# K transposed before its split, softmax reciprocals through DRAM, and gate work moved beside another product, in a two-layer encoder kernel

## The chip, the cores and the metric

The kernel runs on one core of a Trainium2 chip, as one program. The metric is the device time of one execution in microseconds (us). Times of before are the median of three runs; the profile is of one further execution of the same program.

## The reference, cut to what matters

Two layers of an encoder are applied to 1024 prompt tokens and 256 sample tokens (model width 1024, head width 64, all float32). In every layer a normalised, modulated input goes through head groups, an output projection, and a squared-ReLU MLP of width 4096.

```python
def gqa_full(q, k, v):
    ...
    def block(qblk):
        s = jnp.einsum('bqhgd,bkhd->bhgqk', qblk, k,
                       preferred_element_type=jnp.float32) * (Dh ** -0.5)
        p = jax.nn.softmax(s, axis=-1)
        return jnp.einsum('bhgqk,bkhd->bqhgd', p, vf)
```

Layer 0 has dilated-window attention (heads A) and grouped-query attention (heads B); both end as exp(scores) times V, divided by a row sum. Layer 1 has a bidirectional mLSTM (heads C) and a gated MLP over 128-token chunks (heads D): per token an input gate and a forget gate (running sums and maxima over the sequence), an output gate `sigmoid(o)` on the normalised mLSTM output, and `gelu(u) * mixed(v)` in D.

## The kernel before, in words

All 1280 tokens lie in NT = 10 tiles of P = 128 tokens. PE products of float32 data are made of three passes over a high and a low half (`split`, L91: ACT rounds to the high half, DVE subtracts to get the low one; names end in h and l): high by high, low by high, high by low. Weights come in raw through SP's DMA queue and are split the same way, on DVE or, where a caller asks, on POOL (`w_piece`, L269). The program is laid out by a scheduler from the order in which the code issues work; `after(...)` (L82) keeps what is issued within it behind named instructions, on all engines. Each engine then runs its own list in order.

The stages, with their place in the span: `start` (norms, layer-0 projections, and the K of heads B), `attention0` (366 to 806 us), `mix_out(0)` (output projection), `mlp_up(0)`, `mlp_down(0)` (to about 1757), `proj1` (layer-1 projections, 1757 to 2115), `mlstm` (to 2251), `mix_out(1)` (to about 2400), `mlp_up(1)` and `mlp_down(1)`.

**K.** For each tile `k_split` (L334) lays K out twice side by side on POOL, its high half first and then, by a subtraction, its low half. `k_trans` (L341) transposes both halves of both heads (four transposes by the identity, `M<-ident,kd`) and copies the high ones out on ACT (L349, `KH`), the low ones on DVE (L350, `KL`). That is 10 tiles in `start` and 40 in `attention0`.

**Attention items.** There are 80 items, one for each token tile and pair of query heads: 40 of heads B, then four units of 10 of heads A; the last two tiles of every ten are the short sample ones. For an item, `scores` (L566) makes scores and their exponentials with row sums, `trans` (L608) transposes the exponentials (L615, `T<-ident,pe`) and takes the reciprocals of the two sums (L623, `rc`), and `pv` (L627) multiplies by V into the PSUM tile `O`, of which there is one; DVE multiplies by the reciprocals (L648, `ot`) and a DMA stores the result (L650, `oT`). The three steps of an item are issued one item apart. The reciprocals stand one to a token, on partitions, and are needed along a row: POOL copies them out to 128 columns (L625, `rb`), PE transposes (L638), ACT copies to `rs` (L640). `mix_out(0)` loads the stored rows as its operand (L823).

**mlp_up.** Four pairs of weight groups q. Pairs 2 and 3 use a seven-product scheme; `up(P, w, x)` (L858) makes one product, 12 matmuls of 512 columns (4 blocks by three passes). S1 to S4 are sums of weights which DVE makes and splits (`w_sums` L980, `prepare` L999), and T1 to T4 are sums of the input.

**proj1.** `chunks` (L287) walks through specs in order: v (256 columns), og (output gates, 512 columns, L307), vg (gate inputs and D's values, 544 columns, L314), u (512 columns, L359), each over 10 tiles, 24 matmuls of 512 columns to a tile for og and u. In `vg`'s wake stand the mixing of D (L1335, transposes of `scr`) and the gates of C (`gates` L1426): a long chain on DVE of adds, scans (L1473 to L1497), exponentials on ACT and small products on PE (L1535, `tr<-R,selp`, decays). It is a generator of which `u` takes three steps per tile.

**mlstm and mix_out(1).** `w_out` (L713) is a generator of weight pieces for the next output projection; `weights(t)` (L1698) takes one at t = 0, 2, 4 and 6, and POOL makes their low halves. In `mix_out(1)`, `split(t)` (L748) splits the projection's operand (`hTh`, `hTl`), squares and sums the mLSTM output, and multiplies with the gates; at t = 0 the first half of the product and then the four weight pieces that are left are issued.

Of the kernel before, what the change touches and what calls it, by code (L numbers as in the profile page):

```python
# [9 lines left out]
F32 = mybir.dt.float32  # L10
# [39 lines left out]
class Trunk:  # L50
# [283 lines left out]
    def k_split(self, kd, k):  # L334

        src = k.rearrange("p (h d) -> p h d", d=HD).unsqueeze(2).to_broadcast([P, 2, 2, HD])
        self.nc.gpsimd.tensor_copy(kd[:, :, 0].bitcast(F32R), src)
        self.nc.gpsimd.tensor_sub(kd[:, :, 1], src, kd[:, :, 0])
        return kd

    def k_trans(self, kd, ps, K, t):  # L341

        nc = self.nc
        ps = ps.rearrange("p (b n) -> p b n", n=P)
        for h in range(2):
            for i in range(2):
                nc.tensor.transpose(ps[:, 2 * i + h], kd[:, h, i].rearrange("p a d -> p (a d)"), self.ident)
        sl = slice(t * P, (t + 1) * P)
        nc.scalar.activation(K[0][:, :, sl], ps[:, 0:2], AF.Copy, scale=-0.125)  # L349
        nc.vector.tensor_scalar(K[1][:, :, sl], ps[:, 2:4], -0.125, None, op0=OP.mult)  # L350
# [4 lines left out]
    def start(self):  # L355
# [4 lines left out]
        with ExitStack() as s:  # L360
# [95 lines left out]
            def kvb(t, z):  # L456
                z = z[0]
                r = norm(z[:, :P], 2)
                a = self.rope(z[:, :P], tabs["cosBk"], tabs["sinBk"], 2, 16, t)
                scaled(a, r, 2)  # L460
                kds[t] = self.k_split(t2p.tile([P, 2, 2, 2, HD], F32, name="kd", bufs=3), a[:, :P])
                for u in ([t - 2] if t > 1 else []) + ([t - 1, t] if t == NT - 1 else []):
                    self.k_trans(kds[u], self.ps("tr"), self.KB, u)
                v = self.t2()
                nc.scalar.activation(v[:, :P], z[:, P:2 * P], AF.Copy)
                nc.sync.dma_start(self.zd["vb"][:, t], v[:, :P])
# [31 lines left out]
    def attention0(self):  # L498
        nc, I, tc = self.nc, self.I, self.tc
        self.oT = [self.dram.tile([P, KB, P], F32, name=f"oT{t}") for t in range(NT)]  # L500
        with ExitStack() as s:
# [22 lines left out]
            def k_unit(u):  # L524
# [9 lines left out]
                def step(t, kt):  # L534
                    self.k_trans(self.k_split(ap.tile([P, 2, 2, 2, HD], F32, name="kd"), kt), self.ps("M"), K, t)
                    if t in (3, 7):
                        h = t // 4
                        off = 96 * (1 - h)
                        for X in K:
                            b = X.rearrange("p h (b n) -> p h b n", n=P)  # L540
                            for i in range(2):
                                nc.gpsimd.tensor_copy(b[:, i, NT + h].rearrange("p (c n) -> p c n", n=32),
                                                      self.f(b[:, i, 4 * h:4 * h + 4, off:off + 32]))
# [64 lines left out]
            def trans(it, h):  # L608
# [11 lines left out]
                if h == 1:  # L620
                    rc = ap.tile([P, 2], F32, name="rc", bufs=4)
                    for i in range(2):
                        nc.vector.reciprocal(rc[:, i:i + 1], it["sum", i])  # L623
                    rb = it["rb"] = ap.tile([P, 2, HD], F32, name="rb2", bufs=2)
                    nc.gpsimd.tensor_copy(rb, rc.unsqueeze(2).to_broadcast([P, 2, HD]))  # L625

            def pv(it):  # L627
# [9 lines left out]
                r = self.ps("M")  # L637
                nc.tensor.transpose(r[:, :P], it["rb"].rearrange("p h d -> p (h d)"), self.ident)  # L638
                rs = ap.tile([P, P], F32, name="rs", bufs=2)
                nc.scalar.activation(rs, r[:, :P], AF.Copy)  # L640
# [7 lines left out]
                nc.vector.tensor_mul(ot, o[:, :P], rs)  # L648
# [5 lines left out]
            for i, it in enumerate(items):  # L654
                it["last"] = i >= len(items) - 2
# [79 lines left out]
    def mix_out(self, l):  # L735
        nc = self.nc
        with ExitStack() as s:
# [10 lines left out]
            def split(t):  # L748
# [5 lines left out]
                else:  # L754
# [3 lines left out]
                    nc.scalar.activation(sq.rearrange("p (b n) -> p b n", b=4), o, AF.Square)  # L758
# [4 lines left out]
                    v = self.rawp.tile([P, 1088], F32, name="raw", bufs=4)[:, :512].rearrange("p (b n) -> p b n", b=4)  # L763
                    nc.vector.tensor_mul(v.rearrange("p b (h d) -> p b h d", d=HD), ov,
                                         r.rearrange("p (b h) -> p b h", h=2).unsqueeze(3).to_broadcast([P, 4, 2, HD]))
                    nc.vector.tensor_mul(v, v, g)
                    st["v", t] = v
                if t == 0:
                    if l == 1:
                        mm(0, range(4))  # L770
                    for _ in self.w_out:
                        pass
# [102 lines left out]
    def mlp_up(self, l):  # L875
# [6 lines left out]
        with ExitStack() as s:  # L882
# [161 lines left out]
            for q in range(2, self.N_PAIRS):  # L1044
# [37 lines left out]
                P5 = self.ps("u")  # L1082
# [6 lines left out]
                P3 = self.ps("u")  # L1089
                self.up(P3, w("S4"), mov["B22"])  # L1090
                nc.vector.tensor_add(C12, C12, P3)
# [182 lines left out]
    def proj1(self, keep):  # L1274
# [5 lines left out]
        with ExitStack() as s:  # L1280
# [26 lines left out]
            def og(t, z):  # L1307

                o = t2()
                nc.scalar.activation(o, z[0], AF.Sigmoid)  # L1310
                nc.gpsimd.tensor_mul(o, o, mh)
                nc.sync.dma_start(self.ogd[t * P:(t + 1) * P], o)

# [45 lines left out]
            def u(t, z):  # L1359
# [4 lines left out]
                if t == 0:  # L1364
                    late.pop("mix")()
                else:
                    u_trans(t - 1)
                for _ in range(3):
                    next(gen["g"], None)

            def u_trans(t):
                x = late.pop(("u", t))
                ps = self.ps("tr").rearrange("p (b n) -> p b n", n=P)
                for b in range(4):
# [6 lines left out]
            specs = [(w[:, 1280:1536], 256, None, v), (w[:, 1536:2048], 512, None, og),  # L1381
                     (I["w_vg"], 544, None, vg), (w[:, 2080:2592], 512, load_mix, u)]
# [3 lines left out]
            for _ in gen["g"]:  # L1386
                pass
# [164 lines left out]
    def mlstm(self):  # L1552
# [3 lines left out]
        with ExitStack() as s:  # L1556
# [141 lines left out]
            def weights(t):  # L1698
                if t % 2 == 0 and t < 8:
# [156 lines left out]
```

## Time and profile before

| | us |
|---|---|
| median of 3 runs | 3194.86 |
| lowest and highest run | 3188.7, 3201.8 |
| profiled execution, its own time | 3196.31 |
| its span, first to last instruction | 3194.5 |

| engine | busy us | share | instructions |
|---|---|---|---|
| PE | 3111.5 | 97% | 18045 |
| DVE | 1880.6 | 59% | 3339 |
| ACT | 1429.1 | 45% | 2905 |
| POOL | 784.7 | 25% | 828 |

The first two engines' shares are of the whole span. Time in a view is counted from the span's start. In a row of a timeline, the bracket at the end gives the time for which the engine was idle before, and the instruction that ended the wait. The granted TensorE clock (PEclk) is given as a share of the full 2.4 GHz; 0.50 is 1.2 GHz. Its mean over the span is 0.988.

### The profile page before, as it was taken

How to read it: one execution, taken by the hardware profiler on the slowest of the kernel's cores; microseconds unless marked ns; L12 is line 12 of the kernel's file. 1: busy time of each engine (PE TensorE's matmuls, PEld its weight loads, DVE VectorE, ACT ScalarE, POOL GpSimd, SP SyncE). 2: the span in 40 equal slices, each digit the busy share in tenths (PEclk: the TensorE clock that was granted, in tenths of full speed). 3: DMA queues.
4: the chain of work that ended last, by engine and by line, in shares of the span. 5: the costliest groups of instructions: out<-in, count | busy, mean ns of one | idle time of the engine just before them, and what ended most of it. 6: DMA issues, size and time to landing. Idle time of an engine off the chain costs nothing. (4 is left out here: it accounts for less than half of the span.)

```text
span 3194.5 us, 49043 instructions
## 1 busy us (share of the span) xinstructions
PE 3111.5 (97%) x18045; PEld 2582.4 (81%) x18045; DVE 1880.6 (59%) x3339; ACT 1429.1 (45%) x2905; POOL 784.7 (25%) x828
## 2 busy tenths in 40 slices
PE   7999999999999999999999999999899999999998
PEld 4777788888777888888888896889777888888887
DVE  4632266667668767644488135137678767654556
ACT  3411366677444444443366235125454444443344
POOL 2421122353005455400000221202014455500000
PEclk8999999999999999999999999999899999999999
DMA  8536622121634666765567313212643666675567
GB/s 271 170 131 213 198 75 80 47 70 48 208 99 159 218 216 224 249 211 172 177 212 235 111 54 102 63 39 67 182 164 122 215 223 223 228 243 172 177 217 230
DMA packets 312789, 520.42 MB, mean 163 GB/s; under 512 B 43093, under 2 KB 172293, under 8 KB 312421
## 3 DMA queue, kind: packets, MB, share of 16 engines
q1 hardware_dynamic: 312405, 516.89, 49.8%
q8 instruction: 142, 2.33, 0.3%
q14 instruction: 98, 0.80, 0.1%
q0 software_dynamic: 144, 0.39, 0.0%
HBM read 359.71 MB, written 157.48 MB: 162 GB/s over the span
## 5 line engine op out<-in xcount | busy, mean ns | idle before, releaser
L1133 PE MATMUL d<-w1l,sh 128*128 128x512 f32 x1120 | 436.4, 390 | 1.0 <-DVE w1l L94 1.0
L1134 PE MATMUL d<-w1h,sl 128*128 128x512 f32 x1120 | 436.0, 389 | 0.0
L1132 PE MATMUL d<-w1h,sh 128*128 128x512 f32 x1120 | 435.4, 389 | 0.0
L94 DVE TENSOR_TENSOR w1l<-raw,w1h 128x512 fp32r<-128x512 f32 x444 | 363.2, 827 | 119.4 <-ACT w1h L93 116.6
L864 PE MATMUL u<-hTh,w1l 128*128 128x512 f32 (+1 forms) x1056 | 359.2, 340 | 8.5 <-DVE w1l L94 8.5
L94 DVE TENSOR_TENSOR sl<-sraw,sh 128x640 fp32r<-128x640 f32 (+2 forms) x240 | 192.2, 802 | 296.2 <-ACT sh L93 295.9
L864 PE MATMUL u<-hTh,w1h 128*128 128x512 f32 (+1 forms) x1056 | 359.5, 340 | 3.3 <-ACT H L1018 1.7
L864 PE MATMUL u<-hTl,w1h 128*128 128x512 f32 (+1 forms) x1056 | 359.3, 340 | 0.1
L93 ACT ACTIVATE w1h<-raw 128x512 fp32r<-128x512 f32 x444 | 274.6, 622 | 140.3 <-PE u L864 102.7
L93 ACT ACTIVATE sh<-sraw 128x640 fp32r<-128x640 f32 (+2 forms) x240 | 168.6, 704 | 373.4 <-PE d L1133 348.6
L283 PE MATMUL z<-wh,hTh 128*128 128x512 f32 (+2 forms) x800 | 277.4, 364 | 2.1 <-ACT wh L93 1.0
L283 PE MATMUL z<-wl,hTh 128*128 128x512 f32 (+2 forms) x800 | 271.3, 356 | 1.1 <-DVE wl L94 0.5
L285 PE MATMUL z<-wh,hTl 128*128 128x512 f32 (+2 forms) x800 | 270.7, 355 | 1.6 <-DVE hTl L165 1.6
L1133 PEld LDWEIGHTS d<-w1l,sh 128*128 128x128 f32 x1120 | 210.2, 188 | 45.6 <-DVE w1l L94 1.8
L1132 PEld LDWEIGHTS d<-w1h,sh 128*128 128x128 f32 x1120 | 210.3, 188 | 43.5
L1134 PEld LDWEIGHTS d<-w1h,sl 128*128 128x128 f32 x1120 | 210.3, 188 | 43.2
L864 PEld LDWEIGHTS u<-hTh,w1l 128*128 128x128 f32 x1056 | 201.6, 191 | 32.0 <-DVE w1l L94 10.2
L864 PEld LDWEIGHTS u<-hTh,w1h 128*128 128x128 f32 x1056 | 201.8, 191 | 27.0 <-ACT w1h L93 2.1
L864 PEld LDWEIGHTS u<-hTl,w1h 128*128 128x128 f32 x1056 | 201.7, 191 | 22.6 <-DVE hTl L165 1.1
L94 POOL TENSOR_TENSOR wl<-raw,wh 128x1024 fp32r<-128x1024 f32 (+1 forms) x22 | 51.4, 2343 | 526.1 <-ACT wh L93 505.6
L940 POOL TENSOR_TENSOR raw<-raw 128x512 f32<-128x512 f32 x32 | 43.6, 1363 | 543.6 <-DMA raw<-in_w_ff 446.6
L283 PEld LDWEIGHTS z<-wh,hTh 128*128 128x128 f32 x800 | 146.3, 190 | 36.8 <-issue 9.1
(377 smaller groups left out, 6563.6 us busy)
## 6 DMA issues: line engine op xcount, KB each, us to landing
raw<-in_w_ff SPq DMA_DIRECT2D x128, 512.0 KB, 4.1
sraw<-hd SPq DMA_DIRECT2D x192, 320.0 KB, 3.1
wada<-in_w_ada SPq DMA_DIRECT2D x44, 1024.0 KB, 5.4
hd<-H SPq DMA_DIRECT2D x64, 640.0 KB, 4.5
wd<-raw SPq DMA_DIRECT2D x64, 512.0 KB, 3.0
raw<-in_w_ff SPq DMA_DIRECT2D x128, 256.0 KB, 3.8
raw<-wd SPq DMA_DIRECT2D x128, 256.0 KB, 3.2
hd<-part SPq DMA_DIRECT2D x96, 320.0 KB, 3.2
```

Source lines behind the costliest of these rows:

```text
L93: self.nc.scalar.activation(hi, src, AF.Copy)
L94: (eng or self.nc.vector).tensor_sub(lo, src, self.f(hi))
L283: nc.tensor.matmul(o, hi[:, k, sl], w[k][i][:, c], start=first and i == 0, stop=False)
L285: nc.tensor.matmul(o, lo[:, k, sl], w[k][0][:, c], start=False, stop=last)
L864: self.nc.tensor.matmul(o, a[:, k], b, start=(start and k == 0 and i == 0), stop=(stop and k == 3 and i == 2))
L940: v.tensor_sub(B11, B12, B11)
L1132: nc.tensor.matmul(ps, o[0][:, sl], w[0], start=first, stop=False)
L1133: nc.tensor.matmul(ps, o[0][:, sl], w[1], start=False, stop=False)
L1134: nc.tensor.matmul(ps, o[1][:, sl], w[0], start=False, stop=last)
```

## The change

K is laid out twice unsplit, transposed with two transposes, and split behind them: KH is copied out as before, KL is the scaled PSUM less KH. The reciprocals are written to DRAM by a DMA and come back by two broadcast reads as a row for each head. `v` of `mix_out(1)` has other buffers, and the weight pieces left at t = 0 are held behind t = 0's Square and gating product. In `mlp_up`'s pair 2 the product S1 by T1 stands behind S4 by B22. The output gates become 1 / (1 + exp(-o)) by ACT, DVE and DVE. `vg` stands before `og`, the mixing and the gates' steps go beside `og`, and what is left of the gates is issued at `u`'s first tile. The weight pieces in `mlstm` are taken at t = 0, 1, 2 and 3.

```diff
@@ -333,7 +333,5 @@
 
-    def k_split(self, kd, k):
+    def k_twice(self, kd, k):
 
-        src = k.rearrange("p (h d) -> p h d", d=HD).unsqueeze(2).to_broadcast([P, 2, 2, HD])
-        self.nc.gpsimd.tensor_copy(kd[:, :, 0].bitcast(F32R), src)
-        self.nc.gpsimd.tensor_sub(kd[:, :, 1], src, kd[:, :, 0])
+        self.nc.gpsimd.tensor_copy(kd, k.rearrange("p (h d) -> p h d", d=HD).unsqueeze(2).to_broadcast([P, 2, 2, HD]))
         return kd
@@ -343,9 +341,8 @@
         nc = self.nc
-        ps = ps.rearrange("p (b n) -> p b n", n=P)
+        ps = ps[:, :2 * P].rearrange("p (b n) -> p b n", n=P)
         for h in range(2):
-            for i in range(2):
-                nc.tensor.transpose(ps[:, 2 * i + h], kd[:, h, i].rearrange("p a d -> p (a d)"), self.ident)
+            nc.tensor.transpose(ps[:, h], kd[:, h].rearrange("p a d -> p (a d)"), self.ident)
         sl = slice(t * P, (t + 1) * P)
-        nc.scalar.activation(K[0][:, :, sl], ps[:, 0:2], AF.Copy, scale=-0.125)
-        nc.vector.tensor_scalar(K[1][:, :, sl], ps[:, 2:4], -0.125, None, op0=OP.mult)
+        nc.scalar.activation(K[0][:, :, sl], ps, AF.Copy, scale=-0.125)
+        nc.vector.scalar_tensor_tensor(K[1][:, :, sl], ps, -0.125, self.f(K[0][:, :, sl]), op0=OP.mult, op1=OP.subtract)
 
@@ -460,3 +457,3 @@
                 scaled(a, r, 2)
-                kds[t] = self.k_split(t2p.tile([P, 2, 2, 2, HD], F32, name="kd", bufs=3), a[:, :P])
+                kds[t] = self.k_twice(t2p.tile([P, 2, 2, HD], F32, name="kd", bufs=3), a[:, :P])
                 for u in ([t - 2] if t > 1 else []) + ([t - 1, t] if t == NT - 1 else []):
@@ -534,3 +531,3 @@
                 def step(t, kt):
-                    self.k_trans(self.k_split(ap.tile([P, 2, 2, 2, HD], F32, name="kd"), kt), self.ps("M"), K, t)
+                    self.k_trans(self.k_twice(ap.tile([P, 2, 2, HD], F32, name="kd"), kt), self.ps("M"), K, t)
                     if t in (3, 7):
@@ -623,4 +620,8 @@
                         nc.vector.reciprocal(rc[:, i:i + 1], it["sum", i])
-                    rb = it["rb"] = ap.tile([P, 2, HD], F32, name="rb2", bufs=2)
-                    nc.gpsimd.tensor_copy(rb, rc.unsqueeze(2).to_broadcast([P, 2, HD]))
+
+                    d = self.dram.tile([2, P], F32, name=f"rc{it['i'] % 4}")
+                    nc.sync.dma_start(d.rearrange("h p -> p h"), rc)
+                    rs = it["rs"] = ap.tile([P, P], F32, name="rs", bufs=3)
+                    for h in range(2):
+                        nc.sync.dma_start(rs[h * HD:(h + 1) * HD], d[h:h + 1].to_broadcast([HD, P]))
 
@@ -636,6 +637,2 @@
                     vb = [4 * hq + c for c in range(4)] + [4 * (1 - hq) + cq, NT + 1 - hq]
-                r = self.ps("M")
-                nc.tensor.transpose(r[:, :P], it["rb"].rearrange("p h d -> p (h d)"), self.ident)
-                rs = ap.tile([P, P], F32, name="rs", bufs=2)
-                nc.scalar.activation(rs, r[:, :P], AF.Copy)
                 o = self.ps("O")
@@ -647,3 +644,3 @@
                 ot = kp.tile([P, P], F32, name="ot", bufs=2)
-                nc.vector.tensor_mul(ot, o[:, :P], rs)
+                nc.vector.tensor_mul(ot, o[:, :P], it["rs"])
                 q = nc.gpsimd if it["last"] else nc.sync
@@ -654,3 +651,3 @@
             for i, it in enumerate(items):
-                it["last"] = i >= len(items) - 2
+                it["last"], it["i"] = i >= len(items) - 2, i
             first = [0, 40, 50, 60, 70]
@@ -757,3 +754,3 @@
                     sq = self.ps("h")
-                    nc.scalar.activation(sq.rearrange("p (b n) -> p b n", b=4), o, AF.Square)
+                    square = nc.scalar.activation(sq.rearrange("p (b n) -> p b n", b=4), o, AF.Square)
                     r = self.small.tile([P, 8], F32, name="rb", bufs=3)
@@ -762,12 +759,14 @@
                     ov = o.rearrange("p b (h d) -> p b h d", d=HD)
-                    v = self.rawp.tile([P, 1088], F32, name="raw", bufs=4)[:, :512].rearrange("p (b n) -> p b n", b=4)
+                    v = self.t4()[:, :512].rearrange("p (b n) -> p b n", b=4)
                     nc.vector.tensor_mul(v.rearrange("p b (h d) -> p b h d", d=HD), ov,
                                          r.rearrange("p (b h) -> p b h", h=2).unsqueeze(3).to_broadcast([P, 4, 2, HD]))
-                    nc.vector.tensor_mul(v, v, g)
+                    gated = nc.vector.tensor_mul(v, v, g)
                     st["v", t] = v
                 if t == 0:
-                    if l == 1:
-                        mm(0, range(4))
-                    for _ in self.w_out:
-                        pass
+                    with ExitStack() as e:
+                        if l == 1:
+                            mm(0, range(4))
+                            e.enter_context(self.after(square, gated))
+                        for _ in self.w_out:
+                            pass
                 self.load_x(st, 2 * l, t)
@@ -1081,3 +1080,6 @@
                 prepare(q + 1, "A12", "A21")
-                P5 = self.ps("u")
+                P5, P3 = self.ps("u"), self.ps("u")
+                if q == 2:
+                    self.up(P3, w("S4"), mov["B22"])
+                    nc.vector.tensor_add(C12, C12, P3)
                 self.up(P5, w("S1"), mov["T1"])
@@ -1088,5 +1090,5 @@
                 squares(q, 1)
-                P3 = self.ps("u")
-                self.up(P3, w("S4"), mov["B22"])
-                nc.vector.tensor_add(C12, C12, P3)
+                if q > 2:
+                    self.up(P3, w("S4"), mov["B22"])
+                    nc.vector.tensor_add(C12, C12, P3)
                 prepare(q + 1, "S3")
@@ -1309,5 +1311,11 @@
                 o = t2()
-                nc.scalar.activation(o, z[0], AF.Sigmoid)
+                nc.scalar.activation(o, z[0], AF.Exp, scale=-1.0)
+                nc.vector.tensor_scalar(o, o, 1.0, None, op0=OP.add)
+                nc.vector.reciprocal(o, o)
                 nc.gpsimd.tensor_mul(o, o, mh)
                 nc.sync.dma_start(self.ogd[t * P:(t + 1) * P], o)
+                if t == 0:
+                    late.pop("mix")()
+                for _ in range(3):
+                    next(gen["g"], None)
 
@@ -1363,8 +1371,7 @@
                 late["u", t] = x
-                if t == 0:
-                    late.pop("mix")()
-                else:
+                if t > 0:
                     u_trans(t - 1)
-                for _ in range(3):
-                    next(gen["g"], None)
+                else:
+                    for _ in gen["g"]:
+                        pass
 
@@ -1380,4 +1387,4 @@
             w = I["w_in_cd"]
-            specs = [(w[:, 1280:1536], 256, None, v), (w[:, 1536:2048], 512, None, og),
-                     (I["w_vg"], 544, None, vg), (w[:, 2080:2592], 512, load_mix, u)]
+            specs = [(w[:, 1280:1536], 256, None, v), (I["w_vg"], 544, None, vg),
+                     (w[:, 1536:2048], 512, None, og), (w[:, 2080:2592], 512, load_mix, u)]
             for _ in self.chunks(wp, specs, 4, width=544):
@@ -1385,4 +1392,2 @@
             u_trans(NT - 1)
-            for _ in gen["g"]:
-                pass
 
@@ -1698,3 +1703,3 @@
             def weights(t):
-                if t % 2 == 0 and t < 8:
+                if t < 4:
                     with self.after(st["sum"], st["copy"]):
```

The order that this gives on the engines, at three places. The first is PE in `mlp_up`, pair 2 of layer 0 (`u` is the PSUM tile of a product; `w1h2`, `w1l2` are the halves of S1, `w1h3`, `w1l3` those of S4; `hTh`, `hTl` the halves of the input). Before:

```order
L864 MATMUL u_11662<-hTh_9954,w1h2_11548 128x512
L864 MATMUL u_11662<-hTl_9953,w1h2_11548 128x512
L864 MATMUL u_11662<-hTh_9954,w1l2_11549 128x512
L864 MATMUL u_11694<-hTh_9954,w1h3_11612 128x512
L864 MATMUL u_11694<-hTl_9953,w1h3_11612 128x512
L864 MATMUL u_11694<-hTh_9954,w1l3_11613 128x512
```

Now:

```order
L863 MATMUL u_11433<-hTh_9724,w1h3_11382 128x512
L863 MATMUL u_11433<-hTl_9723,w1h3_11382 128x512
L863 MATMUL u_11433<-hTh_9724,w1l3_11383 128x512
L863 MATMUL u_11432<-hTh_9724,w1h2_11318 128x512
L863 MATMUL u_11432<-hTl_9723,w1h2_11318 128x512
L863 MATMUL u_11432<-hTh_9724,w1l2_11319 128x512
```

The two products of 12 matmuls have changed places; each takes its own low half in its third matmul.

The second is DVE in `proj1`, where the gates' chain reaches the chunk decays (`dec`; `gscr` is the gates' work space, `w2` a tile of og or u, `mp` and `ML` the maxima). Before:

```order
L1500 TENSOR_TENSOR ML_20244<-mp_20243,AL_20241 40x10
L1503 TENSOR_TENSOR gscr_18634<-gscr_18634,mp_20243 40x1280
L1362 TENSOR_TENSOR w2_20309<-w2_20309,w2_20204 128x512
L1518 TENSOR_SCALAR gscr_18634<-gscr_18634 40x1280
L1377 COPY w2_20163<-tr_20312 128x512
L1529 TENSOR_TENSOR dec_20362<-mp_20243,ML_20244 40x10
L1523 TENSOR_TENSOR gscr_18634<-gscr_18634,mp_20243 40x1280
```

Now:

```order
L1313 TENSOR_SCALAR w2_19752<-w2_19752 128x512
L1505 TENSOR_TENSOR ML_19689<-mp_19688,AL_19686 40x10
L1508 TENSOR_TENSOR gscr_18404<-gscr_18404,mp_19688 40x1280
L1314 RECIPROCAL w2_19752<-w2_19752 128x512
L1523 TENSOR_SCALAR gscr_18404<-gscr_18404 40x1280
L1313 TENSOR_SCALAR w2_19787<-w2_19787 128x512
L1534 TENSOR_TENSOR dec_19795<-mp_19688,ML_19689 40x10
L1313 TENSOR_SCALAR w2_19837<-w2_19837 128x512
L1314 RECIPROCAL w2_19787<-w2_19787 128x512
```

Behind the maxima stood one product and one copy of `u` ahead of `dec`; now an add of og's, its reciprocal and another add stand there. Five of og's ten reciprocals come ahead of `dec` in all, four more before the last step of the gates, and DVE splits `u`'s weights behind these.

The third is SP's queue at the end of attention (`rc0` to `rc3` are the DRAM tiles of four items in turn, here items 77 to 79 last; `hTl` is the next stage's operand). Before:

```order
L650 DMA oT5_3183<-ot_9785 128x128
L650 DMA oT6_3184<-ot_9854 128x128
L650 DMA oT7_3185<-ot_9903 128x128
L823 DMA hTl_9953<-oT1_3179 128x8x128
L823 DMA hTl_9953<-oT2_3180 128x8x128
```

Now:

```order
L647 DMA oT6_3154<-ot_9630 128x128
L623 DMA rc2_9660<-rc_9657 128x2x1
L623 DMA rc3_9694<-rc_9691 128x2x1
L647 DMA oT7_3155<-ot_9678 128x128
L626 DMA rs_9662<-rc2_9660 64x128 x2
L626 DMA rs_9696<-rc3_9694 64x128 x2
L822 DMA hTl_9723<-oT1_3149 128x8x128
L822 DMA hTl_9723<-oT2_3150 128x8x128
```

Each item has a write and two reads more; the reads of items 78 and 79 stand behind the write of item 79 and the store of item 77, and the next stage's loads behind them all.

## Rows read from the trace of the kernel before

**Rows 1.** PE's waits over the whole span: total, times, longest.

```profile
PE tr L1375 <- DVE w L1362: 3.6, 2, 3.2
PE y L799 <- DVE hTl L94: 1.7, 1, 1.7
PE tr L1535 <- POOL R L1512: 1.5, 1, 1.5
```

**Rows 2.** Windows: us, then each engine's busy time, granted clock, DMA.

```profile
400.00:800.00 400.00, 398.12 (x3721) 330.63 (x3721) 263.87 (x778) 272.62 (x618) 136.65 (x327) 1.00 0.21 63
1968.00:1985.00 17.00, 15.47 (x54) 11.52 (x53) 7.93 (x11) 14.60 (x15) 6.05 (x3) 0.70 0.31 94
2241.00:2265.00 24.00, 17.32 (x61) 14.67 (x60) 14.32 (x23) 10.02 (x16) 3.99 (x3) 0.50 0.62 172
```

**Rows 3.** Timeline of PE in attention: start, duration, line, form, count.

```profile
433.22 1.04 PE L615 MATMUL T<-ident,pe 128*128 128x128 f32 x8
...
703.58 1.52 PE L645 MATMUL O<-pT,vt 128*64 128x128 f32 x22
705.04 0.33 PE L638 MATMUL M<-ident,rb 128*128 128x128 f32 x1
705.29 0.43 PE L645 MATMUL O<-pT,vt 128*64 128x128 f32 x2
```

**Rows 4.** Lines L347 and L650: count, ns at least/median/most, first and last start.

```profile
L347 PE MATMUL M<-ident,kd x160: 272/273/331, 370.0 to 758.2; 128*128 128x128 f32 x160
...
L650 SPq DMA_DIRECT2D oT<-ot x78: 319/320/369, 381.7 to 803.7; - x78
```

**Rows 5.** DMA issues: count, KB each, median us to landing.

```profile
vt<-zva SPq DMA_DIRECT2D x32, 16.0 KB, 1.8
...
gains<-in_qk_norm_g SPq DMA_DIRECT2D x1, 64.0 KB, 8.7
```

**Rows 6.** Timeline of DVE in the last unit: items 70, 71, 78 (reciprocal, product).

```profile
772.67 0.29 DVE L648 TENSOR_TENSOR ot<-O,rs 128x128 f32<-128x128 f32 x1 [0.60 <-issue]
...
777.39 0.29 DVE L648 TENSOR_TENSOR ot<-O,rs 128x128 f32<-128x128 f32 x1 [0.53 <-issue]
...
799.51 0.15 DVE L623 RECIPROCAL rc<-st 128x1 f32<-128x1 f32 x1
...
804.65 0.29 DVE L648 TENSOR_TENSOR ot<-O,rs 128x128 f32<-128x128 f32 x1 [0.34 <-PE O L645]
```

**Rows 7.** Timeline of PE in mlp_up of layer 0, pair 2.

```profile
1005.91 0.50 PE L864 MATMUL u<-hTh,w1h 128*128 128x512 f32 x1 [0.69 <-ACT w1h L93]
...
1013.92 0.79 PE L864 MATMUL u<-hTh,w1l 128*128 128x512 f32 x1 [3.93 <-DVE w1l L94]
```

**Rows 8.** DVE groups by form: count, busy us, mean ns, idle before.

```profile
L623 DVE RECIPROCAL rc<-st 128x1 f32<-128x1 f32 x160 | 24.6, 159 | 37.7 <-ACT pe L605 18.7 <-ACT pe L602 17.8 <-POOL wl L94 0.5
...
L1690 DVE RECIPROCAL de<-de 128x16 f32<-128x16 f32 x10 | 2.5, 252 | 0.3
```

**Rows 9.** Timeline of DVE along the gates' chain beside u.

```profile
1935.73 1.87 DVE L1461 TENSOR_SCALAR gscr<-tr,gbias 40x512 f32<-40x512 f32 x3 [5.50 <-PE tr L1460]
...
1968.67 0.15 DVE L1529 TENSOR_TENSOR dec<-mp,ML 40x10 f32<-40x10 f32 x1
```

**Rows 10.** Timeline of PE from mlstm into mix_out of layer 1.

```profile
2240.12 1.22 PE L1588 MATMUL m<-v,kw 128*128 128x130 f32 x8 [2.30 <-DVE kw L1584]
...
2255.09 1.22 PE L796 MATMUL y<-wh,hTh 128*128 128x512 f32 x2 [3.89 <-ACT hTh L93]
```

**Rows 11.** The same stretch on ACT.

```profile
2251.59 2.94 ACT L93 ACTIVATE wh<-raw 128x1024 fp32r<-128x1024 f32 x3
```

**Rows 12.** The same stretch on DVE.

```profile
2233.22 2.34 DVE L1689 TENSOR_TENSOR de<-de,cols 128x16 f32<-128x16 f32 x1
...
2253.65 4.58 DVE L94 TENSOR_TENSOR wl<-raw,wh 128x1024 fp32r<-128x1024 f32 x3
```

**Rows 13.** The same stretch on POOL.

```profile
2233.18 2.34 POOL L94 TENSOR_TENSOR wl<-raw,wh 128x1024 fp32r<-128x1024 f32 x1
```

More of the change, by code (lines that the diff above doesn't have):

```diff
@@ L1363, in u @@
                 late["u", t] = x
-                if t == 0:
-                    late.pop("mix")()
-                else:
-                    u_trans(t - 1)
-                for _ in range(3):
-                    next(gen["g"], None)
+                if t > 0:
+                    u_trans(t - 1)
+                else:
+                    for _ in gen["g"]:
+                        pass
             def u_trans(t):
```

## The prediction, made before any run of the changed kernel

> **What bounds the kernel.** I read the engines' busy time first: PE is busy for 97% of the span, and DVE, the next, for 59%. In most of attention PE is busy for 398 of 400 us at full clock, DVE and ACT for 264 and 273 [rows 2]. So three things count here: PE work that goes, gaps on PE that come or go, and stretches in which the granted clock is 0.5 (1.2 GHz). The waits of PE show where its gaps lie [rows 1]; the timelines show what stood ahead of the work that came late [rows 6, 7, 9 to 13]; the windows show what the clock did behind the gaps [rows 2]: 0.50 for 24 us around the end of mlstm, 0.70 on average in 17 us of `proj1`, each time after PE had been idle. The sum is made against the profiled execution, 3196.3 us, which stands 1.4 above the median of the runs. From no change, a measurement of this kernel can tell about 0.5%, 16 us.
>
> **K.** Each tile loses two of four transposes. Eight in a row take 1.04 us and the last one lasts about 0.27 [rows 3, 4], so one costs (1.04 - 0.27) / 7 = 0.11. There are 40 tiles in attention (160 transposes [rows 4]) and 10 in `start`: 100 x 0.11 = 11.0 us off PE. POOL's subtraction goes too, and is worth nothing, as other work covers POOL. The low half now waits for ACT's copy of the high one, which comes from the same PSUM tile; DVE has a third of attention free to cover it. Without that cover it would be the 0.4 us of one more ACT copy per tile.
>
> **Reciprocals.** 80 transposes go. In the order of the trace, 45 stand next to other transposes or scores and cost 0.11: 5.0 us. The other 35 split a run of V products: from the last product before to the first behind, PE takes about 0.56 in the row shown (22 products from 703.58, 0.055 apart, the next at 705.29) [rows 3]. I take 0.36 net over 35, since the typical case is 0.46 and neighbouring products stand up to 0.10 apart: 12.6 us. Together 17.6. ACT's and POOL's copies are off the path.
>
> In their place come a write of 256 single elements and two reads. The trace has no such DMA. The nearest are a 16 KB load, 1.8 us to landing, and a broadcast of one row to all partitions, 8.7 [rows 5]; the latter was issued in the first microseconds beside megabyte loads, so I take about 2. An issue costs SP 0.32 [rows 4]. A round trip is then about 0.3 + 2 + 0.6 + 2 = 5 us. Most items have 8 us or more between reciprocal and product. The tightest shown is item 78: reciprocal done at 799.66, product at 804.65 [rows 6]. By the new order its reads stand behind the store of item 77 (about 803.7), so its row lands at 803.7 + 0.3 + 0.3 + 1.8 or a little later, 1.5 to 2 us late. As `O` has one buffer, item 79's V product and the start of the next stage wait with it: **+2 us**, 0 if the reads come sooner, +9 by the 8.7 row. SP's next loads move back by as much, under the 11 us that the first tile of `mix_out` takes.
>
> The Trainium skill ("DMA: Bandwidth & Descriptors", "Rules for kernel authors") says that a strided last dimension makes one descriptor per element, and (its section "Specifications") that under 512 B a transfer is off the line rate. The write is all single elements; no run here shows one. That rule speaks for the slow end, which is a rival below.
>
> **mlp_up, pair 2.** PE began S1's product at 1005.91; the next one, S4's, stalled at its third matmul until 1013.92 for its low half [rows 7], with 10 of its 12 left. Now S4's stands first, while DVE's list still splits S1 first and S4 last of seven. So PE stalls at 1006.4, again until 1013.9, with S1's 12 matmuls still to do: 12 x 0.23 = 2.7 us lost, up to 5 where the clock is at half. I take 3.3 for each of the two layers, **+6.6**; between 0 (DVE gets to S4 sooner with nothing else due) and +11.
>
> **Gates beside output gates.** Before, this stretch lost 3.6 and 1.5 us in waits [rows 1] and, at a mean clock of 0.70 over 17 us, 17 x 0.3 = 5.1 more [rows 2]; the 2.1 us at the mixing stay. That is 10.2 that could go. What comes is ten reciprocals of 128x512 on DVE. One of 1 element per partition takes 159 ns, one of 16 takes 252 [rows 8]: 6.2 ns an element, so 512 take 0.15 + 3.18 = 3.3 us. Were they like a subtraction (three of 128x1024 take 4.58 [rows 12]), it were 0.76. I take 3.3, as the two rows are of the same operation.
>
> The chain from the gates' first add to `dec` took 33 us on DVE [rows 9]. It starts about 10 us into og and now has four more pairs of add and reciprocal in it, 4 x 3.9 = 15.6, and loses `u`'s products and some table loads, so `dec` comes at about 52. Another 8 us passed before PE had what depends on it. So R is there at about 60, while PE reaches the product that reads it in og's eighth tile, after some 48 us (182 matmuls at 0.23 and the small work between): a wait of about 11. Nine reciprocals also stand ahead of DVE's split of `u`'s weights: some 2.5 us more there. With about 3 us at half clock behind it, 16.5 come for 10.2 that go: **+6**. With cheap reciprocals it is -8; a line through two small sizes may also be a quarter short, and with 4.2 us each it is +14.
>
> By the Trainium skill ("VectorE: DVE Perf Modes", "First, the fixed hardware budget") a reciprocal is an iterative divide with a repeat count of 8. Eight times the element part of the subtraction above would be an estimated 4.9 us, and the term some +15; the rows' slope agrees in direction, and decides.
>
> **mlstm and mix_out(1).** PE waited 3.9 us for `hTh` and 1.7 for `hTl` [rows 1, 10], while ACT made three `wh` (2.94 us) and DVE three `wl` (4.58) ahead of them [rows 11, 12]. These move behind: about 2.8 + 1.4 = 4.2 us. POOL's last `wl`, at 2233.18, ran beside a DVE operation on 16 columns that took 2.34 us [rows 12, 13]; it moves to an earlier tile, so the 2.3 us wait for `kw` [rows 10] may go, and with both a part of the 24 us at half clock, which alone held 17.3 us of PE work, 8.6 at full clock [rows 2]. I take **-7**; -4 if only the queues count, -18 if the clock stays up. What PE waits for next there is `wl` of the held pieces, needed only after four blocks of the product.
>
> **Sum:** -11.0 - 17.6 + 2 + 6.6 + 6 - 7 = -21: 3196.3 - 21 = **3175 us**.
>
> **Rivals.**
> - *The new waits hardly appear*: reciprocals cheap or hidden behind vg's and og's tiles, clock up at the end of mlstm. -28.6 + 2 + 5 - 4 - 14 = -40: 3156. For it: the waits removed are real. Against it: the slope in rows 8.
> - *PE's saving in attention is not realised*: without these transposes, PE waits for exponentials, for KL behind KH, or for `ot`. Half of 26 us gone: -8, 3188. For it: ACT is busy for two thirds; against: so little of PE's time there is idle now.
> - *The round trip is slow* (the change's other side). If a read lands in 8.7 us, five items whose reads stand right behind the previous item's store (70, 71, 72, 74, 78) cannot follow each other in the 4.7 us of now (772.67 to 777.39 [rows 6]) but in 0.3 + 0.3 + 0.6 + 8.7 = 9.9: 4 x 5.2, and 9 for item 78. -23 + 30 = +7, and each such gap brings half clock behind it, some 3 us: +22, 3218. It decides from a landing of about 3.5 us on and is above before from 7.
> - *The move of S1's product does nothing*, since DVE's list and not PE's sets the end there: -6.6 more, 3169, within the forecast's own range.
>
> **Numbers.** The forecast as it stands has 0.5 (3164 to 3186), the first rival 0.2, the second 0.2, the slow round trip 0.1. The range is 3152 to 3202, from the first rival to beyond the second, with the upper ends of `mlp_up` and og; most of the slow rival is left out. Faster by over 0.5% means under 3179: two thirds of the forecast and the first rival, 0.54. Slower means over 3211: the slow rival and a little more, 0.10. The rest, 0.36, is within 0.5%.
>
> **What would show it.** L638 gone and PE still without gaps in attention; a reciprocal of 128x512 near 3.3 us, with PE waiting for R in og's eighth tile; a wait of about 7.5 us for `w1l` in pair 2 in place of 3.9; no wait for `hTh` in `mix_out(1)`; reads of `rs` landing in about 2 us. It is wrong if PE waits for `ot` or for `O` through attention, or if reciprocals take under 1 us.

## The result: 404 us more, all but a little of it in attention

| | us |
|---|---|
| before, median of 4 runs | 3195.39 |
| changed, median of 4 runs | 3599.89 (3590.54 to 3607.32) |
| ratio, 95% interval | 1.1262 (1.1245 to 1.1280) |
| changed, profiled execution | 3590.54, span 3588.8, mean clock 0.945 |

One execution of kernel e7 below took 7433 us, in place of 3181 to 3186 for its other six, and is left out of its time.

Stages on PE, from the first matmul of each stage to that of the next (of the last stage to the end of the last matmul) in the timelines of the two profiled executions, whose spans are 394.3 us apart:

| stage | before | changed | difference |
|---|---|---|---|
| to attention's first transpose | 366.2 | 361.8 | -4.4 |
| attention | 439.4 | 825.7 | +386.3 |
| mix_out(0), mlp_up(0) | 535.8 | 539.6 | +3.9 |
| mlp_down(0), proj1 to its last projection | 663.0 | 671.3 | +8.3 |
| q and k, mlstm | 250.7 | 247.5 | -3.2 |
| mix_out(1) to the end | 928.3 | 931.3 | +3.0 |

PE's waits over the whole span of the changed kernel (line, what it waited for, total, times, longest):

```profile
PE O L642 <- DVE ot L645: 161.8, 33, 10.3
PE M L344 <- DVE QS L560: 93.7, 23, 14.9
...
PE tr L1540 <- POOL R L1517: 11.4, 1, 11.4
PE u L863 <- DVE w1l L94: 10.0, 2, 5.2
...
PE u L863 <- ACT w1h L93: 5.3, 2, 2.7
...
PE h L781 <- DVE w L763: 2.8, 2, 2.7
...
PE y L795 <- ACT hTh L93: 2.0, 2, 1.6
```

The first two lines were next to nothing before (0.2 us for `O`) and make 255 us. In a window of attention (us, busy time of PE, its weight loads, DVE, ACT, POOL, then the granted clock) PE, which was busy for 398 of 400 us [rows 2], now has this:

```profile
400.00:1180.00 780.00, 480.01 (x3665) 390.95 (x3664) 258.68 (x797) 264.54 (x560) 94.20 (x224) 0.80 0.27 41
```

PE is busy for 480 of 780 us at a mean clock of 0.80. Over the whole stage it is busy for 509.6 of 825.7 us, 435.4 of 439.4 before: of the 386 us, 312 are idle time, and 74 are busy time, which grew at the lower clock although 160 transposes had gone. PE waits for DVE: `O` for the product `ot`, and K's transposes for the copy `QS` of the transposed queries out of `M`, which stands behind `ot` in DVE's list. DVE's longest wait says why:

```profile
DVE ot L645 <- DMA rs<-rc: 350.3, 55, 14.4
```

And the longest wait of SP's queue, in the same view for SP, leads to the DMA that writes the reciprocals:

```profile
SPq L626 <- DMA rc<-rc: 469.4, 73, 10.3
```

469 us in 73 waits is what SP spends with a read of `rs` (L626) at the head of its list while the write of the same item (L623) has not landed. Two turns of the list, in the timeline of SP (start, duration, line, transfer):

```profile
509.16 0.38 SPq L623 DMA_DIRECT2D rc<-rc  x1
509.64 0.41 SPq L647 DMA_DIRECT2D oT<-ot  x1
517.36 3.51 SPq L626 DMA_DIRECT2D rs<-rc  x2
520.97 0.54 SPq L545 DMA_DIRECT2D q<-zqb  x1
521.60 0.38 SPq L623 DMA_DIRECT2D rc<-rc  x1
522.07 0.42 SPq L647 DMA_DIRECT2D oT<-ot  x1
522.58 0.38 SPq L210 DMA_DIRECT2D wada<-in_w_ada  x1
530.86 1.09 SPq L626 DMA_DIRECT2D rs<-rc  x2
```

The write starts at 509.16, its reads can start at 517.36, 8.2 us later; they and a query load take until 521.5, and only then does the next item's write start, 12.4 us behind the first. Over the 80 items, the write's start stands 8.8 us ahead of its reads in the median (7.1 to 11.9, worked out from the same timeline), and the products follow one another every 10.1 us on average. Before, attention took 439.4 / 80 = 5.5 us an item.

### The profile page after: what moved, and what is told of

It reads as the page before. It is cut to its first block, busy times and chain, and to the rows that moved or that the text cites. A ratio compares the mean times of both kernels' runs of the same rounds, so it can differ in the third digit from the quotient of the medians.

```text
span 3588.8 us, 48744 instructions
## 1 busy us (share of the span) xinstructions
PE 3184.2 (89%) x17865; PEld 2632.5 (73%) x17865; DVE 1897.2 (53%) x3359; ACT 1403.6 (39%) x2818; POOL 735.7 (20%) x698
## 5 line engine op out<-in xcount | busy, mean ns | idle before, releaser
L94 DVE TENSOR_TENSOR w1l<-raw,w1h 128x512 fp32r<-128x512 f32 x444 | 351.6, 801 | 123.6 <-ACT w1h L93 120.5
L642 PE MATMUL O<-pT,vt 128*64 128x128 f32 x1920 | 188.2, 353 | 161.8 <-DVE ot L645 161.8
L642 PEld LDWEIGHTS O<-pT,vt 128*64 128x64 f32 x1920 | 154.4, 182 | 188.5 <-DVE ot L645 158.0
L645 DVE TENSOR_TENSOR ot<-O,rs 128x128 f32<-128x128 f32 x80 | 23.3, 291 | 466.8 <-DMA rs<-rc 350.3
```

Source lines behind the costliest of these rows:

```text
L94: (eng or self.nc.vector).tensor_sub(lo, src, self.f(hi))
L642: nc.tensor.matmul(o[h * HD:(h + 1) * HD, :P], V[:, vb[b], kh * HD:(kh + 1) * HD], it["pT", h][:, b], start=(b == 0), stop=(b == n - 1), t ...
L645: nc.vector.tensor_mul(ot, o[:, :P], it["rs"])
```

## Is it the round trip, and nothing else?

The experiments ran on three chips, each beside runs of before: its median was 3196.42 us for e1 to e4, 3193.76 for e5 to e10 and 3194.55 for e11 to e14. Differences between kernels of two groups can be off by up to 2.7 us for that reason, so they are given by the ratios to before as well.

**e1**: the changed kernel with rows made by transposes as before.

```diff
-                    d = self.dram.tile([2, P], F32, name=f"rc{it['i'] % 4}")
-                    nc.sync.dma_start(d.rearrange("h p -> p h"), rc)
-                    ...
+                    rb = it["rb"] = ap.tile([P, 2, HD], F32, name="rb2", bufs=2)
+                    nc.gpsimd.tensor_copy(rb, rc.unsqueeze(2).to_broadcast([P, 2, HD]))
...
+                nc.tensor.transpose(r[:, :P], it["rb"].rearrange("p h d -> p (h d)"), self.ident)
+                nc.scalar.activation(rs, r[:, :P], AF.Copy)
```

> The changed kernel with the reciprocals made into rows as before (POOL copy, transpose, ACT copy), all its other parts kept. Theory A, the round trip through DRAM alone costs the time: outside attention the changed kernel's stages sum to +7.6 us against before (start -4.4, proj1 +8.8, mlstm -3.3, the rest +6.5), and K's 80 transposes in attention are worth -8.8, so about 3194 us (3186 to 3202). Theory B, the new order of K (low half behind ACT's copy of the high half) also stalls attention: 3230 us or more.

Measured: 3202.25 us, ratio to before 1.0016 (1.0007 to 1.0025). Theory A holds: without the round trip 398 us of the 404 are gone. The time lies just above A's range and 8 us over the sum of the stages, mostly in q, k and mlstm, 253.3 us against 247.5: over the last 18 us of mlstm the mean granted clock is 0.71 here and 1.00 in the changed kernel. Kernels with the same code in this stage show either value (e12 1.00, e4 0.72), so this difference is not put down to the round trip.

**e2**: the kernel before with the round trip alone (the hunks of the change at L623 and in `pv`).

```diff
...
-                nc.vector.tensor_mul(ot, o[:, :P], rs)
+                nc.vector.tensor_mul(ot, o[:, :P], it["rs"])
```

> The kernel before with the reciprocals through DRAM and nothing else of the change. Theory A: SP's queue sets the pace of attention, so the transposes of K that are back do not matter: 3195 + 386 = 3581 us (3560 to 3610). Theory B, half of the loss comes from the other parts: under 3450 us.

Measured: 3567.62 us, ratio 1.1162 (1.1140 to 1.1184). Nearly the whole loss comes back by this one part: 371 us over before, inside the range for A and 13 under its 3581.

## Where does the wait hurt: in the row, or in SP's list?

**e12**: e1, with the write and the reads added for nobody.

```diff
+                    d = self.dram.tile([2, P], F32, name=f"rc{it['i'] % 4}")
+                    nc.sync.dma_start(d.rearrange("h p -> p h"), rc)
+                    rx = ap.tile([P, P], F32, name="rx", bufs=3)
+                    for h in range(2):
+                        nc.sync.dma_start(rx[h * HD:(h + 1) * HD], d[h:h + 1].to_broadcast([HD, P]))
```

> Kernel e1 (rows by transposes, all else as changed) with the write of 256 pieces and the two reads as well, into a tile that nobody uses: SP's list has the waits of the changed kernel, but no product waits for the row. Theory Q, SP's list sets the pace: reads wait 8.8 us for their write, and query loads, stores and the next write queue behind them, some 10.8 us an item against 6 of PE's work: 3450 to 3600 us. Theory L, it is the way of the row to the product that costs: 3202 to 3230 us.

Measured: 3583.58 us, ratio 1.1216 (1.1191 to 1.1241), with this wait in SP's list:

```profile
SPq L627 <- DMA rc<-rc: 484.8, 73, 10.0
```

Theory Q. No product reads these rows, and the kernel is still nearly as slow as the changed one (ratio 1.1216 against 1.1262). What stands behind the waiting reads is late instead; DVE's longest wait is now

```profile
DVE ot L650 <- DMA oT<-ot: 376.0, 59, 19.4
```

that is, for a free `ot` buffer, whose store (L652 in this kernel) queues behind the reads.

**e4**: the changed kernel, the write from ACT's queue.

```diff
-                    nc.sync.dma_start(d.rearrange("h p -> p h"), rc)
+                    nc.scalar.dma_start(d.rearrange("h p -> p h"), rc)
```

> The changed kernel with the write of the reciprocals issued by ACT's queue; the two reads stay on SP. Theory A1, the wait stands in SP's list, where the next item's write and all loads queue behind the reads that wait for this item's write: with the write off that list a write is issued at once, the row is there some 13 us (8.8 write, 1.1 issue of the reads, 2.9 landing) behind the reciprocals, and items take about 7.5 us in place of 10: 3320 us (3230 to 3420). Theory A2, the length of the round trip alone sets the pace, wherever it waits: 3550 us or more.

Measured: 3467.57 us, ratio 1.0849 (1.0829 to 1.0869): between the two, a miss for both. The write now starts 0.7 us behind the reciprocals in the median, 8.7 in the changed kernel. But its reads still start 9.0 us behind it in the median, and SP's list still waits for it, less often:

```profile
SPq L626 <- DMA rc<-rc: 275.8, 54, 9.7
```

So taking the next write from behind the waiting reads gives 132 us back, a third of the loss. The rest was not taken apart: the reads still wait in SP's list, and stores and query loads still stand behind them, as in e12.

## Why does a write of one kilobyte take 9 us?

**e5**: 128 pieces of 8 bytes. **e6**: two pieces of 512 bytes.

```diff
-                    nc.sync.dma_start(d.rearrange("h p -> p h"), rc)
+                    nc.sync.dma_start(d.rearrange("h p -> (h p)").rearrange("(p h) -> p h", h=2), rc)
```

```diff
+                    rw = ap.tile([2, P], F32, name="rw", bufs=4)
+                    nc.vector.tensor_scalar(rw, it["pT", 1][0:2, 0], rc[0:2, 1:2], None, op0=OP.mult)
-                    nc.sync.dma_start(d.rearrange("h p -> p h"), rc)
+                    nc.sync.dma_start(d, rw)
```

> The changed kernel, but each partition's two reciprocals go to DRAM as one piece of 8 bytes, 128 pieces in place of 256 of 4 bytes; the reads are unchanged, so each query is scaled by another one's factor. Theory P, the write's 8.8 us is a price for each piece, about 2 fixed and 6.8 for 256: landing about 5.4 us, SP's loop 3.4 us shorter, 3590 - 80 x 3.4 = 3320 us. Theory F, it is a fixed latency of a small write to DRAM: still 8 to 9 us, 3570 to 3610.

> The changed kernel, but the write takes two rows of 128 numbers (512 bytes each, from two partitions, made by one more DVE operation on 2 x 128 elements); what comes back as factors is then not the reciprocals. Theory P (a price per piece): 2 pieces, landing 2 to 3 us; SP's loop (0.4 + 2.5 + 1.1 + 0.5 + 0.4, about 5 us) is under the 6 us of an item, attention near its length before: 3200 to 3260 us. Theory F: landing 8 to 9 us and 3570 to 3610.

Measured, one execution each: e5 3269.16 us, e6 3194.53. SP's waits for the write in e5:

```profile
SPq L626 <- DMA rc<-rc: 161.7, 67, 5.0
```

A third of the 469. In the timeline of SP, a write of e5 with its reads and the next write:

```profile
513.34 0.38 SPq L623 DMA_DIRECT2D rc<-rc  x1
516.48 1.09 SPq L626 DMA_DIRECT2D rs<-rc  x2
517.62 0.58 SPq L623 DMA_DIRECT2D rc<-rc  x1
```

3.1 us from write to reads; the median over 80 is 4.2, 8.8 in the changed kernel. In e6 SP has no wait for the write among its longest at all; there, a write, a store, the reads and a query load:

```profile
510.66 0.25 SPq L625 DMA_DIRECT2D rc<-rw  x1
511.73 0.33 SPq L649 DMA_DIRECT2D oT<-ot  x1
512.15 1.25 SPq L628 DMA_DIRECT2D rs<-rc  x2
514.51 0.33 SPq L545 DMA_DIRECT2D q<-zqb  x1
```

1.5 us here, 2.5 in the median. Theory F is out, and theory P holds in the main: from 256 pieces to 128 the write gets (8.8 - 4.2) / 128 = 0.036 us shorter for each piece less. That is no exact price (128 times it is more than the 4.2 us left), and in e6 other transfers stand between, so 2.5 is at most what the write takes. The amount of data is the same 1 KB in all three, so fewer pieces are also longer ones, and the runs do not tell the number from the length. e5 came out below its 3320, its landing being 4.2 in place of 5.4, and e6 a little below its 3200.

The packets on the DMA queues, in the changed kernel and then in e5:

```profile
DMA packets 347349, 525.75 MB, mean 146 GB/s; under 512 B 67413, under 2 KB 206853, under 8 KB 346981
DMA packets 337109, 525.75 MB, mean 161 GB/s; under 512 B 57173, under 2 KB 196613, under 8 KB 336741
```

Those under 512 B differ by 10240 = 80 x 128: a write has 128 packets more where its pieces are single elements. The Trainium skill's rule in "DMA: Bandwidth & Descriptors", "Rules for kernel authors" (one descriptor per element where the last dimension is strided) is borne out by this; it gives no price. In e5's trace the 128 packets of a write start within 1.5 us of its issue in the median, and the reads only some 2.3 us behind the last of them. In the changed kernel the packets of 4 bytes, as far as they can be told from others, start within about 1.7 us, the reads at 8.8. So most of the price lies between the start of the packets and the landing; why it grows with the pieces there, no run shows.

## The other parts, one by one

**e3**: the kernel before with K's part alone (`k_twice`, `k_trans`).

```diff
...
-            for i in range(2):
-                nc.tensor.transpose(ps[:, 2 * i + h], kd[:, h, i].rearrange("p a d -> p (a d)"), self.ident)
+            nc.tensor.transpose(ps[:, h], kd[:, h].rearrange("p a d -> p (a d)"), self.ident)
...
```

> The kernel before with K transposed before its split and nothing else. Prediction's term: -11 us, about 3184 (3180 to 3188). Rival, the wait for KH eats the gain: 3193 or more.

Measured: 3184.41 us, ratio 0.9964 (0.9950 to 0.9977), 12 us less. The term holds.

**e7**: e3 and the two parts around the end of mlstm.

```diff
-                if t % 2 == 0 and t < 8:
+                if t < 4:
...
+                            e.enter_context(self.after(square, gated))
```

> The kernel before with K's part and the two parts around the end of mlstm (weight pieces at t = 0 to 3; the four pieces of mix_out(1) held behind the Square and the gating). Prediction's terms: -12 as measured for K alone, and -7 (from -4 to -18): 3177 us. Rival, from the changed kernel's trace: PE waits less for hTh (2.0 in place of 3.9) but for the sums of squares and for the gating product instead, so the tail is worth 0 to -3: 3181 to 3184.

Measured: 3184.53 us, ratio 0.9970 (0.9958 to 0.9982): 0.1 above e3, 2 by the ratios. So the two parts gain nothing, and the time is just above the rival's range. The timeline of PE there:

```profile
2229.51 1.16 PE L1587 MATMUL m<-v,kw 128*128 128x130 f32 x8 [0.78 <-DVE kw L1583]
...
2242.07 1.22 PE L795 MATMUL y<-wh,hTh 128*128 128x512 f32 x2 [1.63 <-ACT hTh L93]
...
2253.05 1.12 PE L781 MATMUL h<-ident,w 128*128 128x128 f32 x4 [3.38 <-DVE w L763]
```

The wait for `kw` fell from 2.30 to 0.78 and that for `hTh` from 3.89 to 1.63 [rows 10]; a new one of 3.38 for the gating product (L763) stands in their place.

**e10**: e7 and S1's product behind S4's.

```diff
+                if q == 2:
+                    self.up(P3, w("S4"), mov["B22"])
+                    nc.vector.tensor_add(C12, C12, P3)
                 self.up(P5, w("S1"), mov["T1"])
```

> The kernel e7 and S1's product moved behind S4's. Prediction's term +6.6 for the two layers; by the changed kernel's trace PE's two stalls there are 2.7 + 5.2 us in each layer in place of 0.7 + 3.9, and the last 12 matmuls follow, so +2.6 to +3.3 in each: 5 to 7 us above e7. Rival: 0, the longer wait replaces one elsewhere.

Measured: 3190.14 us, ratio 0.9990 (0.9981 to 0.9998): 5.6 above e7, on the same chip. In the changed kernel's timeline of PE the two stalls read

```profile
1391.09 0.50 PE L863 MATMUL u<-hTh,w1h 128*128 128x512 f32 x1 [2.70 <-ACT w1h L93]
...
1397.04 0.79 PE L863 MATMUL u<-hTh,w1l 128*128 128x512 f32 x1 [5.21 <-DVE w1l L94]
```

where the product that came first had waited 0.69 and the other 3.93 [rows 7].

**e13**: e1 without the gates' reciprocals. **e14**: e3 and the new order of proj1, with Sigmoid.

```diff
-                nc.vector.reciprocal(o, o)
```

In e14, set against the changed kernel's output gates:

```diff
-                nc.scalar.activation(o, z[0], AF.Exp, scale=-1.0)
-                nc.vector.tensor_scalar(o, o, 1.0, None, op0=OP.add)
-                nc.vector.reciprocal(o, o)
+                nc.scalar.activation(o, z[0], AF.Sigmoid)
```

> Kernel e1 with the reciprocals of the output gates left out (the gate is then 1 + exp(-o)). If these ten of 3.35 us are what makes R late in og's eighth tile, five of them go from its chain, 16.7 us, more than the wait of 11.4: no wait there, and 3202 - 12 = 3190 us (3186 to 3193), the time of e10. Rival, the chain is late by itself: wait 5 us or more, above 3195.

> The kernel before with K's part and the new order of proj1 (vg ahead of og, mixing and gates beside og), but with the output gates by ACT's Sigmoid as before. Without reciprocals on DVE the gates' chain is done before og ends; the waits of 3.6 and 1.5 us and the half clock behind them, 5.1, may go: 3184 - 8 = 3176 us (3172 to 3182). Rival: ACT loads a table (1.28 us) for each change between Sigmoid, Exp and Ln and the chain comes late again: 3184 to 3195.

Measured: e13 3197.90 us, ratio 1.0009 (1.0000 to 1.0018); e14 3189.22, ratio 0.9981 (0.9972 to 0.9990), 4.8 above e3 (5 by the ratios). Both times lie in the rival's range. PE's wait for R, in e13 and then in e14:

```profile
PE tr L1539 <- POOL R L1516: 10.2, 1, 10.2
```

```profile
PE tr L1533 <- POOL R L1510: 11.1, 1, 11.1
```

In e13 the chain is shorter: from the gates' first add to `dec` it takes 31.8 us, 41.9 in e1. But the scheduler also put R earlier in PE's list, behind 144 of og's matmuls in place of 182 (38 x 0.233 = 8.9 us of PE's time). e14's rival blamed table loads: e14 has 23 of them, e1 and e13 have 16. But e13 waits for R nearly as long as e14, so the loads are not shown to be the cause.

The ten reciprocals are worth 4.4 us by the medians (3202.25 - 3197.90) and 2 by the ratios, whose intervals overlap. e1 stands 12.1 us above e10, 8 by the ratios, and the two differ by the gates alone; in their profiles half of it lies in q, k and mlstm, where the clock over the last 18 us is 0.71 in e1 and 1.00 in e10. The gates' own stage tells more: mlp_down(0) with proj1 takes 670.7 to 672.5 us in the six kernels that have the new gates (the changed one, e1, e4, e5, e6, e12) and 660.1 to 665.8 in the six that have the old ones (before, e2, e3, e7, e10, e11), 8.5 us less on average. Why the scheduler takes the chain to be some 10 us shorter than it is was not tried.

## A version below both

**e11**: e3, with the round trip, and the reciprocals laid along rows by DVE before they are written.

```diff
+                    rc = ap.tile([P, 32], F32, name="rc", bufs=2)
+                    for i in range(2):
+                        nc.vector.reciprocal(rc[:, 16 * i:16 * i + 16], it["sum", i].to_broadcast([P, 16]))
+                    rt = ap.tile([P, 32], F32, name="rt", bufs=3)
+                    nc.vector.transpose(rt, rc)
...
+                    for h in range(2):
+                        nc.sync.dma_start(d[h].rearrange("(g e) -> g e", e=32), rt[16 * h:P:32])
```

> The kernel before with K's part and reciprocals by way of DRAM, but laid along rows by DVE first (a transpose of 32x32 blocks, 16 equal columns for each head), so that a write has 8 pieces of 128 bytes in two DMAs in place of 256 of 4. Theory P (price per piece, as e5 and e6 showed): landing about 2.5 us, the round trip is hidden in nearly all items, and without the 80 transposes attention ends as much earlier as in e6 against e1, 8.6 us: 3184 - 8 = 3176 us (3172 to 3184). Rival: the two DMAs more on SP and DVE's 0.5 us more in each item lengthen attention: 3190 to 3220.

Measured: 3176.45 us, ratio 0.9943 (0.9930 to 0.9955), 18 us below before and 8 below e3 (7 by the ratios, whose intervals just overlap). DVE's two new groups (mean ns of one behind the busy time), PE's wait for `O`, and a window of attention:

```profile
L620 DVE RECIPROCAL rc<-st 128x16 f32<-128x16 f32 x160 | 38.0, 243 | 18.6 <-ACT pe L602 12.5 <-ACT pe L599 5.8
...
L622 DVE STREAM_TRANSPOSE rt<-rc 128x32 f32<-128x32 f32 x80 | 16.7, 209 | 2.0
```

```profile
PE O L645 <- DVE ot L648: 2.6, 3, 1.9
```

```profile
400.00:780.00 380.00, 372.25 (x3585) 309.16 (x3583) 281.27 (x858) 255.53 (x548) 92.38 (x220) 1.00 0.29 84
```

PE is busy for 98% of this window at full clock again, and `ot` holds it up for 2.6 us in all.

## Why the prediction was wrong, point by point

- **Round trip: wrong, and it decides.** The step that failed is the price of the write: "so I take about 2" us, from a 16 KB load and a broadcast. It measured 8.8. The reads were near the 2 us that were taken (2.0 at least, 2.9 in the median from the issue of the second to the product). The nearest row was no bound: a load of 32 pieces of 512 bytes says nothing of 256 pieces of 4 bytes. The prediction's own sign of being wrong came true: PE waits for `O` through attention.
- **SP's list: missed.** The prediction priced a late row, with 8 us of slack in most items (71 of 80 in the trace of before; the tightest is item 79 with 2.9 us, not item 78), and so +2 us. It did not count that an in-order list which waits 8.8 us for a write in each item cannot turn faster than 8.8 + 1.1 + the issues of a load and a store, over 10 us. e12 shows that this alone makes the loss. The rival of a slow round trip had the place, but chained items through stores and the read alone, in five items, and so 3218 us at a chance of 0.1. That its 8.7 us, taken for a read, is close to what the write took is chance.
- **K: right.** -11 forecast, -12 measured.
- **80 transposes of the reciprocals: work right, gain too large.** -17.6 forecast. With a cheap write it was 8 us (e11 against e3; 7 by the ratios). In attention PE's busy time fell by 21.3 us (428.9 to 407.6) and its idle time rose by 7.9 (2.8 to 10.7), 13.4 net; the rest was given back behind it.
- **mlp_up: right,** +6.6 forecast, +5.6 measured.
- **Gates: chain and wait right, cost a little low.** A reciprocal of 128x512 came to 3.3 us as forecast, in the groups of DVE by form:

```profile
L1314 DVE RECIPROCAL w<-w 128x512 f32<-128x512 f32 x10 | 33.4, 3345 | 0.1
...
L1313 DVE TENSOR_SCALAR w<-w 128x512 f32<-128x512 f32 x10 | 5.2, 521 | 3.4 <-ACT w L1312 3.4
```

  The chain to `dec` took 41.9 us, 42 by the forecast's figures (from 10 us into og to 52), and PE's wait for R came to 11.4, 11 was forecast. The part cost 8.5 us in its stage, +6 was forecast. That the wait goes with the reciprocals does not hold: in e13 and e14, without them, PE asks for R as much sooner. The +15 that the prediction names for reciprocals of 4.9 us does not fit its own step (0.9 us more each makes +8, so 1.6 more about +20); at 3.3 us measured, nothing hangs on it.
- **mlstm and mix_out(1): wrong,** -7 forecast, nothing gained: the waits moved on to the gating product, which the prediction did not name as next.

With a cheap write too the gain would not have come: e6, which has all the other parts, took 3194.53 us in its one execution, inside the stated range, but 0.8 above before on its chip in place of 21 below.

## What to carry to other kernels

Here a small write took longer the more pieces it had, with the same 1 KB. Where a DMA's innermost pieces are single elements, try to make the data lie along rows on the chip first (here one DVE transpose of 0.21 us) and send few pieces. SP's list ran in order, and a read that waited for the write's landing held up everything behind it. With such a list, count the waits of one turn of the list against the time of one turn of the work, before any slack of a single transfer.

## What was not expected of the hardware

1 KB written to DRAM took 8.8 us as 256 pieces, 4.2 as 128 and at most 2.5 as two, though the packets start within about 1.7 us. Leaving out the reciprocals made the gates' chain 10 us shorter but did not bring PE's wait for its result down (11.4 to 10.2 us), since the order on PE moved with it.
